# Host-side layouts for the arrays of a hybrid encoder step, and the place of the weight splits during its recurrence

## The chip, the cores and the metric

The kernel runs on one core of a Trainium2 chip, as one program and one launch. The metric is the device time of one execution in microseconds (us). The kernel before was run three times: 2982.29, 2989.22 and 2990.96 us, median 2989.22. One execution, of 2981.34 us, was recorded by the profiler, and all rows of the profile below are of that one.

## The reference

One inference step of a two-layer encoder, over a prompt of 512 tokens and a sample of 32 tokens with 1024 channels, in fp32. Each layer is: half a SwiGLU, a mixer, cross-attention to a memory of 256 tokens, half a SwiGLU; each of these ends with a LayerNorm over the scaled residual.

```python
def post_norm(x, sub, g, b):
    return layer_norm(ALPHA * x + sub, g, b)
def swiglu(x, w_up, w_down):
    gate, up = jnp.split(x @ w_up, 2, axis=-1)
    return (jax.nn.silu(gate) * up) @ w_down
```

The mixer of layer 0 is a gated linear recurrence beside chunkwise retention; that of layer 1 is RWKV-7 time mixing, a recurrence over a state of 64x64 per head and 16 heads. Outputs are the tokens, the memory's keys and values for both layers, and the states of all recurrences after the prompt and after the sample.

## The kernel before

**Layout.** Activations stand with channels on the 128 partitions: a tile is [128, 8, n], channel c*128+p at partition p of chunk c. The tokens are split into two halves, A (prompt 0 to 255, n = 256) and B (prompt 256 to 511 and the 32 of the sample, n = 288), with tiles XA, XHA, XLA and XB, XHB, XLB: the value, its rounded high part, and the rest. A matmul keeps fp32 accuracy by three passes: high weight times high x, low weight times high x, high weight times low x.

**Weights.** They are streamed in granules of 128 output columns: 1024x128 numbers, 512 KB. `_load` brings a granule by one DMA on SyncE's queue into one of three raw tiles `wr` (at most two ahead per stream). `_split` makes the two parts in one of five slots W: ScalarE the high part (L486), then VectorE (L408) or GpSimd (L412) the low one, raw minus high. `ett` chooses the engine by when a planner's clock has either free, with a lag of 300 in GpSimd's disfavour. `linear` then issues 24 matmuls for each granule and half, all through line L395.

**Order.** The program is recorded by coroutines, one for each half, one for the memory's keys and values (`mem_kv`), one for stored states. A planner gives each instruction a planned start, which becomes its priority in each engine's queue; a task with a lower `band` is placed ahead of all with a higher one. Each engine then works strictly in its own order. Lines below L500 are helpers: L395 matmul, L400 transpose by TensorE (an identity `identt` as an operand), L408 and L412 two-input operations of VectorE and GpSimd, L432 a three-input one, L443 copy, L451 memset, L486 ScalarE's activation, L491 every DMA.

**Stages.** Eight stages follow: ffn00, mix0, xa0, ffn10 of layer 0, then ffn01, mix1, xa1, ffn11. The rows of x arrive as [tokens, channels] and are transposed by TensorE in `load_x` (tiles HHA, HHB, HLB), y is transposed back in `store_x`; `mem_kv` transposes the memory, and its keys and values, with TensorE beside ffn00 and mix0; `attend` transposes the sample's cached keys; the RWKV state is transposed on its way in and out.

**The recurrence of mix1.** `wkv` cuts A and B into nine blocks: four of 64 tokens each, and the sample's 32. For each block `wkv_prep` builds small 64x64 matrices by matmuls (two chunks a block) and hands them through DRAM (`dn`) to GpSimd; `wkv_solve` is a triangular solve of 31 steps on GpSimd, two instructions a step, on tiles P and LC; the result goes through DRAM (`dz`) into tile W_114 (W_111 after the change), and `wkv_chain` carries the state on with matmuls (ax). GpSimd itself issues the DMAs P<-dn, dz<-LC and W<-dz. Meanwhile the other stages of the half that isn't in the recurrence run on with their own weight granules, through two slots, W_3 and W_4.

Of the kernel before, what the change touches and what calls it, by code (L numbers as in the profile page):

```python
# [14 lines left out]
ALU = mybir.AluOpType  # L15
# [358 lines left out]
class Kern(Clock):  # L374
# [186 lines left out]
    def setup_weights(self):  # L561
        self.slots = Res(self, [self.wslot(k) for k in range(NSLOT)])
        self.raws = Res(self, [self.pool.tile([128, 8, 128], F32, name="wr%d" % k) for k in range(NRAW)])
        self.streams, self.go = [], False
        self.kept = [0, 0]
# [37 lines left out]
    def _load(self, s):  # L603
# [10 lines left out]
        self.dma(r[:, :kc, :m], ap.rearrange("(c p) m -> p c m", p=128))  # L614
# [4 lines left out]
    def _split(self, s):  # L619
# [82 lines left out]
def load_params(K):  # L702
# [7 lines left out]
    groups = [[("ln_g", i["ln_g"].rearrange("l i (r p) -> (l i r) p", p=128), 64),  # L710
               ("ln_b", i["ln_b"].rearrange("l i (r p) -> (l i r) p", p=128), 64)]]
    one = [("mu", i["l1_mu"].rearrange("i (r p) -> (i r) p", p=128), 48)]
    for n in ("w0", "a0", "k_k", "k_a", "gn_g", "gn_b"):
        one.append((n, i["l1_" + n].rearrange("(r p) -> r p", p=128), 8))
    one.append(("r_k", i["l1_r_k"].rearrange("(r a) b -> r (a b)", a=2), 8))
    groups.append(one)
    two = [("conv_w", i["l0_conv_w"].rearrange("j (r p) -> (j r) p", p=128), 16)]
    for n in ("conv_b", "lru_ba", "lru_bx", "lru_lambda", "ret_gn_g", "ret_gn_b"):
        two.append((n, i["l0_" + n].rearrange("(r p) -> r p", p=128), 4))
    two.append(("lru0", i["state_lru0"].rearrange("b (r p) -> (b r) p", p=128), 4))  # L720
    two.append(("conv0", i["state_conv0"].rearrange("b j (r p) -> (b j r) p", p=128), 12))
    two.append(("shift1", i["state_shift1"].rearrange("b j (r p) -> (b j r) p", p=128), 8))
    groups.append(two)
    tot = sum(n for g in groups for _, _, n in g)
    K.pv = K.pool.tile([128, tot], F32, name="pv")
    col = 0
    for g in groups:
        blk = yield from K.ar.take((128,))
        st, = blk
        r = 0  # L730
        for n, ap, k in g:
            K.dma(st[r:r + k], ap)
            VEC[n] = col + r
            r += k
        ps = yield from K.aux.take()
        K.tr(ps[:, :r], st[:r])
        K.vcopy(K.pv[:, col:col + r], ps[:, :r])
        K.aux.give(ps)
        blk.free()
        col += r  # L740
# [22 lines left out]
def program(K):  # L763
# [6 lines left out]
    def add(ap, m0, m1, k0, k1):  # L770
        for m in range(m0, m1, 128):
            gran.append((ap[k0:k1, m:m + 128], (k1 - k0) // 128, 128))
# [89 lines left out]
def half_main(K, h):  # L862
# [20 lines left out]
    yield from store_x(K, h)  # L883
# [11 lines left out]
def load_x(K, h):  # L895

    nc, n = K.nc, h.n
    h.x = K.slot("X" + h.name, [128, 8, n])
    h.xh = K.slot("XH" + h.name, [128, 8, n], F32R)
    h.xl = K.slot("XL" + h.name, [128, 8, n], F32R)  # L900
    st = K.slot("HH" + h.name, [128, 8 * n])
    parts = [(K.i["x_prompt"][0, h.c0 + t * 128:h.c0 + t * 128 + 128], t * 128, 128, st[:, t * 1024:t * 1024 + 1024])
             for t in range(2)]
    if h is K.B:
        parts.append((K.i["x_sample"][0], 256, 32, K.slot("HLB", [128, 8 * n])[:, :1024]))
    for src, t0, m, st in parts:
        K.dma(st[:m], src)
    K.go = True
    yield
    for src, t0, m, st in parts:  # L910
        for q in range(2):
            ps = yield from K.aux.take()
            p3 = ps.rearrange("p (a b) -> p a b", a=4)
            for c in range(4):
                K.tr(p3[:, c, :m], st[:m, (q * 4 + c) * 128:(q * 4 + c) * 128 + 128])
            d = (slice(None), slice(q * 4, q * 4 + 4), slice(t0, t0 + m))
            K.act(h.xh[d], p3[:, :, :m])
            K.tt(h.xl[d], p3[:, :, :m], h.xh[d].bitcast(F32), ALU.subtract)
            K.vcopy(h.x[d], p3[:, :, :m])
            K.aux.give(ps)  # L920
            yield
    event(K, "x", h.name).fire(K)
    yield K.done()


def store_x(K, h):
    parts = [(K.o["y_prompt"][0, h.c0 + t * 128:h.c0 + t * 128 + 128], t * 128, 128) for t in range(2)]
    if h is K.B:
        parts.append((K.o["y_sample"][0], 256, 32))
    blks = []  # L930
    for dst, t0, m in parts:
        blk = yield from K.ar.take((1024,))
        blks.append(blk)
    for q in range(2):
        for (dst, t0, m), blk in zip(parts, blks):
            st = blk.aps[0][:m, q * 512:q * 512 + 512]
            ps = yield from K.aux.take()
            for c in range(4):
                K.tr(ps[:m, c * 128:c * 128 + 128], h.x[:, q * 4 + c, t0:t0 + m])
            (K.vcopy if t0 == 128 else K.act)(st, ps[:m])  # L940
            K.aux.give(ps)
            K.dma(dst[:, q * 512:q * 512 + 512], st)
    yield
    yield K.done()
    for blk in blks:
        blk.free()


def store_states(K):
# [5 lines left out]
    blk = yield from K.ar.take((128,))  # L955
    st, = blk
    ps = yield from K.aux.take()
    K.tr(ps[:48, :128], K.ov)
    K.vcopy(st[:48], ps[:48, :128])
    K.aux.give(ps)  # L960
    o = K.o
    yield K.done()
    for nm, a, r in (("p_conv", 0, 12), ("s_conv", 12, 12)):
        K.dma(o[nm].rearrange("b j (r p) -> (b j r) p", p=128), st[a:a + r])
    for nm, a, r in (("p_lru", 24, 4), ("s_lru", 28, 4)):
        K.dma(o[nm].rearrange("b (r p) -> (b r) p", p=128), st[a:a + r])
    for nm, a, r in (("p_shift", 32, 8), ("s_shift", 40, 8)):
        K.dma(o[nm].rearrange("b j (r p) -> (b j r) p", p=128), st[a:a + r])
    yield K.done()
    blk.free()  # L970
# [97 lines left out]
def post_ln(K, h, l, e, whole=False, final=False):  # L1068
# [53 lines left out]
def mem_kv(K):  # L1122
# [10 lines left out]
    for l in range(2):  # L1133
        for ap in (i["xa_k"][l], i["xa_v"][l]):
            for j in range(8):
                gran.append(ap[:, j * 128:j * 128 + 128])
# [7 lines left out]
    for t in range(2):  # L1144
        K.dma(st, i["mem_prompt"][0, t * 128:t * 128 + 128])
        p3 = ps.rearrange("p (a b) -> p a b", a=4)
        for q in range(2):
            for c in range(4):
                K.tr(p3[:, c], st[:, (q * 4 + c) * 128:(q * 4 + c) * 128 + 128])
            hi, lo = mh[:, q * 4:q * 4 + 4, t * 128:t * 128 + 128], ml[:, q * 4:q * 4 + 4, t * 128:t * 128 + 128]  # L1150
            K.act(hi, p3)
            K.tt(lo, p3, hi.bitcast(F32), ALU.subtract)
# [4 lines left out]
    for g, ap in enumerate(gran):  # L1157
# [3 lines left out]
        dst = K.o["mem_v" if kind else "mem_k"][l, 0].rearrange("(t p) h d -> p t (h d)", p=128)  # L1161
# [920 lines left out]
```

## Time and profile before

| | |
|---|---|
| runs | 2982.29, 2989.22, 2990.96 us |
| profiled execution | 2981.34 us, of which the span of the trace is 2979.5 us |
| mean granted TensorE clock | 0.952 |
| TensorE busy in 1000 to 1300 us | 300.00 of 300 us |
| TensorE busy in 1300 to 1500 us | 192.04 of 200 us |
| TensorE busy in 1500 to 1850 us | 338.79 of 350 us |
| GpSimd busy, all | 909.1 us, 424.20 of them between 1850 and 2450 us |
| HBM traffic, mean | 110 GB/s |

Engines are PE (TensorE's matmuls), PEld (its weight loads), DVE (VectorE), ACT (ScalarE), POOL (GpSimd) and SP (SyncE). A row of a view by groups names the line, engine, operation, what is written <- what is read, the shape and the count, then busy us and the mean ns of one, then the idle time of that engine just before these instructions and what ended it. Neighbouring matmuls overlap, so a group's busy time is less than count times mean. A row of the timeline gives start and length in us, and in brackets the idle time ahead of it with its releaser. A row of the chain of waits gives a start, a length and what that piece of the end's path was spent on. The recurrence lies between about 1880 and 2440 us.

### The profile page before, as it was taken

The page shows a single profiled execution, that of the slowest core. Times are in us where ns is not written, and L with a number is a line of the kernel's source. Part 1 is how long each engine was busy: PE and PEld are TensorE (multiplying, and loading weights), DVE is VectorE, ACT ScalarE, POOL GpSimd, SP SyncE. Part 2 cuts the span into 40 slices and gives each one's busy share as a digit, 9 for nine tenths or more (in the row PEclk, how much of TensorE's full clock was granted, in tenths as well). Part 3 has the DMA queues.
Part 4 walks back from the last instruction along what each step waited for, and adds up shares of the span by engine and source line. Part 5 has one row for each costly group of instructions (what it writes and reads, how often), then busy time and mean ns, then how long its engine had stood idle before and what let it go on. Part 6 is the DMA issues. An engine that isn't in the chain of part 4 may idle for free.

```text
span 2979.5 us, 54689 instructions
## 1 busy us (share of the span) xinstructions
PE 2809.6 (94%) x22456; PEld 2701.7 (91%) x22456; DVE 1765.9 (59%) x3094; ACT 1276.8 (43%) x2182; POOL 909.1 (31%) x1201
## 2 busy tenths in 40 slices
PE   8999998999998999998999899799779989999998
PEld 8999998898898999998999899578678878999997
DVE  5333436677767333356345655877588657765665
ACT  4323233665555222234234443444345454654444
POOL 2000104433314000023001212588577764241311
PEclk9999999999999999999999999799678889999999
DMA  6443443223232332322346554133122245546563
GB/s 184 124 120 116 134 117 107 77 75 90 89 98 71 100 89 82 93 79 85 86 138 184 143 145 128 38 90 98 42 70 80 75 115 167 149 144 181 167 174 94
DMA packets 611035, 330.56 MB, mean 111 GB/s; under 512 B 29032, under 2 KB 603840, under 8 KB 610784
## 3 DMA queue, kind: packets, MB, share of 16 engines
q1 hardware_dynamic: 603328, 310.93, 36.3%
q0 software_dynamic: 7456, 16.13, 2.0%
q8 instruction: 176, 2.88, 0.4%
q14 instruction: 75, 0.61, 0.1%
HBM read 313.09 MB, written 13.92 MB: 110 GB/s over the span
## 4 chain that ended last, share of the span: by engine, by line
PE 71%; DVE 11%; POOL 7%; ACT 5%; issue 3%; DMA 3%; SPq 0%; DVEq 0%; ACTq 0%; POOLq 0%
PE mm L395 65%; PE ax L395 5%; POOL LC L412 2%; POOL P L412 2%; DVE W L408 2%; ACT arena L486 2%; DVE arena L408 1%; DVE arena L432 1%; ACT W L486 1%; PE ax L400 1%; DVE XA L408 1%; DMA wr<-in_ffn_up 1%; POOL arena L412 1%; ACT L2043 1%; DVE XB L408 1%
## 5 line engine op out<-in xcount | busy, mean ns | idle before, releaser
L486 ACT ACTIVATE W<-wr 128x1024 fp32r<-128x1024 f32 (+1 forms) x558 | 577.7, 1038 | 725.8 <-PE mm L395 587.1
L408 DVE TENSOR_TENSOR W<-wr,W 128x1024 fp32r<-128x1024 f32 (+1 forms) x453 | 562.4, 1244 | 541.2 <-ACT W L486 536.8
L395 PE MATMUL mm<-XHB,W 128*128 128x288 f32 x3840 | 581.0, 300 | 15.4 <-ACT XHB L486 4.8
L395 PEld LDWEIGHTS mm<-XHB,W 128*128 128x128 f32 x3840 | 528.3, 190 | 24.1 <-ACT XHB L486 5.8
L395 PE MATMUL mm<-XHA,W 128*128 128x256 f32 x3840 | 530.8, 288 | 16.4 <-ACT XHA L486 6.6
L395 PEld LDWEIGHTS mm<-XHA,W 128*128 128x128 f32 x3840 | 494.8, 193 | 25.9 <-ACT XHA L486 10.8
L412 POOL TENSOR_TENSOR W<-wr,W 128x1024 fp32r<-128x1024 f32 (+1 forms) x105 | 253.9, 2419 | 659.7 <-ACT W L486 652.7
L395 PE MATMUL mm<-XLB,W 128*128 128x288 f32 x1984 | 313.6, 298 | 1.4 <-DVE XLB L408 1.4
L395 PE MATMUL mm<-HHB,W 128*128 128x288 f32 x1920 | 291.6, 302 | 9.7 <-ACT W L486 3.5
L395 PE MATMUL mm<-XLA,W 128*128 128x256 f32 x1984 | 290.5, 285 | 2.3 <-POOL XLA L412 2.3
L395 PE MATMUL mm<-HHA,W 128*128 128x256 f32 x1920 | 271.7, 290 | 14.5 <-DVE XA L408 5.0
L395 PEld LDWEIGHTS mm<-XLB,W 128*128 128x128 f32 x1984 | 281.2, 190 | 3.4 <-DVE XLB L408 1.9
L395 PEld LDWEIGHTS mm<-HHB,W 128*128 128x128 f32 x1920 | 268.7, 192 | 12.8 <-ACT W L486 4.5
L395 PEld LDWEIGHTS mm<-HHA,W 128*128 128x128 f32 x1920 | 250.7, 194 | 20.5 <-ACT W L486 5.3
L395 PEld LDWEIGHTS mm<-XLA,W 128*128 128x128 f32 x1984 | 261.6, 191 | 4.5 <-POOL XLA L412 2.5
L486 ACT ACTIVATE arena<-mm 128x256 f32<-128x256 f32 (+4 forms) x292 | 112.6, 388 | 308.2 <-PE mm L395 289.9
L432 DVE SCALAR_TENSOR_TENSOR arena<-mm,arena 128x288 f32<-128x288 f32 (+1 forms) x176 | 77.3, 439 | 161.7 <-PE mm L395 143.7
L395 PE MATMUL mm<-HLB,W 128*128 128x288 f32 x896 | 142.7, 299 | 0.0
L395 PE MATMUL mm<-HLA,W 128*128 128x256 f32 x896 | 129.9, 284 | 0.0
L412 POOL TENSOR_TENSOR SUMA<-XA 128x256 f32<-128x256 f32 x16 | 14.4, 901 | 377.3 <-DVE XA L408 360.7
L395 PEld LDWEIGHTS mm<-HLB,W 128*128 128x128 f32 x896 | 129.3, 192 | 0.1
L412 POOL TENSOR_TENSOR LC<-LC,P 128x66 f32<-128x66 f32 (+24 forms) x279 | 122.7, 440 | 20.6
(430 smaller groups left out, 3769.6 us busy)
## 6 DMA issues: line engine op xcount, KB each, us to landing
wr<-in_ffn_up SPq DMA_DIRECT2D x246, 512.0 KB
wr<-in_ffn_down SPq DMA_DIRECT2D x96, 448.0 KB
wr<-in_l_w_rkv SPq DMA_DIRECT2D x48, 512.0 KB
wr<-in_ffn_down SPq DMA_DIRECT2D x40, 512.0 KB
wr<-in_l_w_in SPq DMA_DIRECT2D x24, 512.0 KB
wr<-in_l_w_out SPq DMA_DIRECT2D x24, 512.0 KB
wr<-in_xa_q SPq DMA_DIRECT2D x24, 512.0 KB
wr<-in_xa_o SPq DMA_DIRECT2D x24, 512.0 KB
```

The source lines that it names most:

```text
L395: self.nc.tensor.matmul(out, lhsT, rhs, start=start, stop=stop)
L400: self.nc.tensor.transpose(out, in_, self.ident[k0:k0 + k, k0:k0 + k])
L408: self.nc.vector.tensor_tensor(out, a, b, op=op)
L412: self.nc.gpsimd.tensor_tensor(out, a, b, op=op)
L432: self.nc.vector.scalar_tensor_tensor(out, a, s, b, op0=op0, op1=op1)
L486: return self.nc.scalar.activation(out, a, f, bias=bias, scale=scale, **kw)
L2043: nc.scalar.preload_act_table_set(name)
```

## The change

Two parts. First, arrays are laid out on the host as the DMAs want them, before the launch and after it: a weight granule is contiguous, with 4 KB for each partition instead of eight pieces of 512 bytes; x, the memory, the vectors, the cached keys, the small RWKV weights and the RWKV state come as they stand in SBUF; y, the memory's keys and values, the small states and the RWKV state are stored as they stand there. The transposes of these by TensorE, and the copies behind them, are left out; those of the memory's values stay, since attention needs values in both layouts. Second, between the start and the end of `wkv`'s tasks (`K.busy`) a split is recorded with band -1, and its low part is always VectorE's.

```diff
         ap, kc, m = g[k][:3]
         self.end = self.now
-        self.dma(r[:, :kc, :m], ap.rearrange("(c p) m -> p c m", p=128))
+        self.dma(r[:, :kc, :m], ap)
...
+        band = self.band
+        if self.busy:
+            self.band = -1
         self.act(wh[:, :kc, :m], r[:, :kc, :m])
-        self.ett(wl[:, :kc, :m], r[:, :kc, :m], wh[:, :kc, :m].bitcast(F32), ALU.subtract, GSP)
+        if self.busy:
+            self.tt(wl[:, :kc, :m], r[:, :kc, :m], wh[:, :kc, :m].bitcast(F32), ALU.subtract)
+        else:
+            self.ett(wl[:, :kc, :m], r[:, :kc, :m], wh[:, :kc, :m].bitcast(F32), ALU.subtract, GSP)
+        self.band = band
...
-    yield from store_x(K, h)
...
-            for c in range(4):
-                K.tr(p3[:, c, :m], st[:m, (q * 4 + c) * 128:(q * 4 + c) * 128 + 128])
...
+    for c in range(0, 8, 2):
+        (K.dma, K.adma)[c // 2 % 2 if h is K.A else 0](h.x[:, c:c + 2], K.i["x"][:, c:c + 2, h.c0:h.c0 + n])
     K.go = True
     yield
...
+    for c in range(0, 8, 2):
+        u = slice(c, c + 2)
+        K.act(h.xh[:, u], h.x[:, u])
+        K.tt(h.xl[:, u], h.x[:, u], h.xh[:, u].bitcast(F32), ALU.subtract)
+        yield
...
             first(c)
             second(c)
+            if final:
+                K.dma(K.o["y"][:, c, h.c0:h.c0 + n], x[:, c])
...
         K.act(a, ps[:, :256])
+        K.gdma(K.o["mem_v" if kind else "mem_k"][l, j * 128:j * 128 + 128], a)
         if kind == 0:
             K.gdma(K.kt[l][j * 128:j * 128 + 128], a)
+            yield K.done()
+            continue
...
-        K.dma(r3[:, 0], K.i["cache_mem_k"][l, 0, :, hd].rearrange("(c p) d -> p c d", p=128))
+        K.dma(r3[:, 0], K.i["cache_k"][l, hd])
...
+    K.busy = True
     evs = [K.spawn(f(K, w), 0, p)
            for f, p in ((wkv_prep, -1), (wkv_solve, -2), (wkv_load, -3), (wkv_chain, -4), (wkv_norm, -1))]
     for e in evs:
         yield e
+    K.busy = False
...
-                yield from state_out(K, w, Yn, K.o["p_wkv"][0])
+                K.gdma(K.o["p_wkv"], Yn[0:64])
```

What this moves is seen in the order of the instructions. On TensorE at the program's start, before:

```order
L400 MATMUL ax_67<-identt,HHA_93 128x128 x4
L400 MATMUL ax_69<-identt,HHA_93 128x128 x4
L400 MATMUL ax_70<-identt,HHA_93 128x128 x4
L400 MATMUL ax_67<-identt,HHA_93 128x128 x4
L395 MATMUL mm_63<-XHA_91,W_1_71 128x256
L400 MATMUL ax_68<-identt,HHB_101 128x128 x4
L400 MATMUL ax_69<-identt,HHB_101 128x128 x4
L395 MATMUL mm_64<-XHA_91,W_2_72 128x256
L395 MATMUL mm_63<-XHA_91,W_1_71 128x256 x15
```

and of the change, at the same place:

```order
L395 MATMUL mm_63<-XHA_91,W_1_71 128x256 x16
L395 MATMUL mm_63<-XLA_92,W_1_71 128x256 x8
L395 MATMUL mm_64<-XHA_91,W_2_72 128x256 x16
L395 MATMUL mm_64<-XLA_92,W_2_72 128x256 x8
L395 MATMUL mm_65<-XHB_100,W_1_71 128x288 x16
```

The transposes of x ahead of and between the first linears are gone; the first granules are used whole, one after the other.

On GpSimd behind the solve of the recurrence's first block, where its result is handed on (dz, then W_114) and the next block's matrices are fetched (P<-dn), before:

```order
L412 TENSOR_TENSOR LC_7380<-LC_7380,P_115_17677 128x8
L491 DMA dz_17682<-LC_7380 256x1x32 x4
L412 TENSOR_TENSOR W_3_73<-wr_76,W_3_73 128x1024
L412 TENSOR_TENSOR W_4_74<-wr_77,W_4_74 128x1024
L491 DMA W_114_17676<-dz_17682 32x8x32 x4
L451 MEMSET LC_7380 128x256
L491 DMA P_115_17677<-dn_17681 32x1024 x4
L451 MEMSET LC_7380 32x8 x4
L412 TENSOR_TENSOR W_4_74<-wr_77,W_4_74 128x1024
L412 TENSOR_TENSOR P_115_17677<-LC_7380,P_115_17677 128x31
```

and of the change:

```order
L412 TENSOR_TENSOR LC_7233<-LC_7233,P_112_17512 128x8
L491 DMA dz_17517<-LC_7233 256x1x32 x4
L491 DMA W_111_17511<-dz_17517 32x8x32 x4
L451 MEMSET LC_7233 128x256
L491 DMA P_112_17512<-dn_17516 32x1024 x4
L451 MEMSET LC_7233 32x8 x4
L412 TENSOR_TENSOR P_112_17512<-LC_7233,P_112_17512 128x31
```

The three splits of weights have left GpSimd's queue. Behind the second and the third solve something else is moved as well: P<-dn stood ahead of dz<-LC there and now stands behind W<-dz.

On TensorE where the recurrence passes from half A to half B: the matmuls on W_111, W_110 (64x64) are the preparation of B's first block, one tile for each of its two chunks, and `ax<-arena,W_114` is the use of the last solve of A. Before:

```order
L395 MATMUL mm_64<-W_111_17673 64x64 x4
L395 MATMUL mm_66<-W_111_17673 64x64 x7
L395 MATMUL ax_68<-wr_78,W_110_17672 32x64 x16
L395 MATMUL ax_68<-arena_79,W_114_17676 128x64 x4
L395 MATMUL ax_69<-wr_78,W_110_17672 64x64 x16
L395 MATMUL ax_68<-W_110_17672,wr_78 64x32 x16
L395 MATMUL mm_64<-W_110_17672 64x64
L395 MATMUL mm_66<-W_110_17672 64x64
L395 MATMUL ax_67<-HLA_16848,centt 128x512
L395 MATMUL mm_64<-W_110_17672 64x64 x7
```

and of the change, where the two chunks stand in W_108 and XHB, and W_111 is the solve's result:

```order
L395 MATMUL mm_63<-W_108_17508 64x64 x7
L395 MATMUL mm_66<-W_108_17508 64x64 x7
L395 MATMUL mm_63<-XHB_19937 64x64 x8
L395 MATMUL mm_66<-XHB_19937 64x64 x8
L395 MATMUL ax_69<-wr_76,W_107_17507 32x64 x16
L395 MATMUL mm_63<-arena_79,bonest 128x512
L395 MATMUL mm_66<-arena_79,bonest 128x512
L395 MATMUL ax_69<-arena_79,W_111_17511 128x64 x4
```

The second chunk's preparation stood behind the second use of the solve's result and now stands ahead of it.

More of the change, by code (lines that the diff above doesn't have):

```diff
@@ L563, in setup_weights @@
         self.raws = Res(self, [self.pool.tile([128, 8, 128], F32, name="wr%d" % k) for k in range(NRAW)])
-        self.streams, self.go = [], False
+        self.streams, self.go, self.busy = [], False, False
         self.kept = [0, 0]
@@ L709, in load_params @@
     K.dma(K.cent, K.c["cent"])
[L710 to L740, printed above, removed]
+    K.pv = K.pool.tile([128, i["pv"].shape[1]], F32, name="pv")
+    K.dma(K.pv, i["pv"])
     K.lng2 = K.pool.tile([128, 64], F32, name="lng2")
@@ L954, in store_states @@
     yield event(K, "shift", "B")
[L955 to L970, printed above, removed]
+    K.dma(K.o["ov"], K.ov)
 def ffn(K, h, l, e):
@@ L1143, in mem_kv @@
     st, = blk
[L1144 to L1152, printed above, removed]
+    for q in range(2):
+        u = slice(4 * q, 4 * q + 4)
+        s4 = st.rearrange("p (c t) -> p c t", c=4)
+        K.dma(s4, i["mem"][:, u])
+        K.act(mh[:, u], s4)
+        K.tt(ml[:, u], s4, mh[:, u].bitcast(F32), ALU.subtract)
         yield K.done()
@@ L1253, in attend @@
     ks = yield from K.keys.take()
-    if c0 == 0:
-        K.act(ks[:, 0], raw[:, 0])
-        K.tt(ks[:, 1], raw[:, 0], ks[:, 0].bitcast(F32), ALU.subtract)
-    else:
-        ps = yield from K.aux.take()
-        p3 = ps.rearrange("p (c n) -> p c n", c=2)
-        for a in range(2):
-            for b in range(2):
-                K.tr(p3[:, b, a * 128:a * 128 + 128], r3[:, 0, a, b * 128:b * 128 + 128])
-        K.act(ks[:, 0], ps)
-        K.tt(ks[:, 1], ps, ks[:, 0].bitcast(F32), ALU.subtract)
-        K.aux.give(ps)
+    K.act(ks[:, 0], raw[:, 0])
+    K.tt(ks[:, 1], raw[:, 0], ks[:, 0].bitcast(F32), ALU.subtract)
     t = K.done()
@@ L1933, in wkv_load @@
         event(K, "load", ci).fire(K)
-def state_out(K, w, Y, dst):
-    blk = yield from K.ar.take((16, 64))
-    st, = blk
-    for q in range(2):
-        ps = yield from w.pl.take()
-        for g in range(8):
-            K.tr(ps[0:64, g * 64:g * 64 + 64], Y[0:64, 8 * q + g])
-        K.act(st[0:64, 8 * q:8 * q + 8], ps[0:64].rearrange("p (g k) -> p g k", g=8))
-        w.pl.give(ps)
-    K.gdma(dst.rearrange("h v k -> v h k"), st[0:64])
-    yield K.done()
-    blk.free()
 def wkv_chain(K, w):
@@ L1959, in wkv_chain @@
         if L == 32:
-            blk = yield from K.ar.take((16, 64))
-            st, = blk
-            yield K.ready([st])
-            K.dma(st[0:64], K.i["state_wkv1"][0].rearrange("h v k -> v h k"))
-            yield K.done()
-            for q in range(2):
-                for g in range(8):
-                    K.tr(b1[0:64, g * 64:g * 64 + 64], st[0:64, 8 * q + g])
-                K.act(Y[0:64, 8 * q:8 * q + 8], b1[0:64].rearrange("p (g k) -> p g k", g=8))
-            blk.free()
+            yield K.ready([Y[0:64]])
+            K.dma(Y[0:64], K.i["wkv0"])
         yield event(K, "load", ci)
@@ L2067 @@
     arrays, ins, outs, consts = {}, {}, {}, {}
-    for name in INS:
-        a = np.ascontiguousarray(inputs[name])
+    for name, a in lay(inputs).items():
+        a = np.ascontiguousarray(a)
         arrays["in_" + name] = a
@@ L2080 @@
     r = run(nc, [arrays], core_ids=[0])
-    return tuple(r.results[0]["out_" + name] for name, _ in OUTS)
+    return tuple(np.ascontiguousarray(a) for a in unlay({name: np.asarray(r.results[0]["out_" + name]) for name, _ in OUTS}))
```

114 lines of the change are left out of this document (57 added, 57 removed), and 3 rows, old and new, of the table INS.

## The prediction

> **What bounds the kernel now.** I read the page's busy shares and chain of waits first, then a table by stages, because a share of the span says little where the limits change from stage to stage.
>
> ```profile
> PE 2809.6 (94%) x22456; PEld 2701.7 (91%) x22456; DVE 1765.9 (59%) x3094; ACT 1276.8 (43%) x2182; POOL 909.1 (31%) x1201
> ...
> q1 hardware_dynamic: 603328, 310.93, 36.3%
> ...
> PE 71%; DVE 11%; POOL 7%; ACT 5%; issue 3%; DMA 3%; SPq 0%; DVEq 0%; ACTq 0%; POOLq 0%
> ```
>
> TensorE is busy 94% and holds 71% of the chain. So what leaves TensorE counts, but only where TensorE is what everything else waits for. The table by stages (stretch, its length, then busy us and instructions of PE, PEld, DVE, ACT, POOL, then clock, DMA share and GB/s) says where:
>
> ```profile
> 0.00:50.00 50.00, 42.31 (x311) 41.02 (x311) 25.44 (x50) 22.39 (x33) 11.18 (x9) 0.97 0.78 226
> 50.00:500.00 450.00, 450.00 (x3607) 449.84 (x3606) 186.71 (x276) 138.50 (x217) 64.45 (x80) 1.00 0.41 119
> 500.00:1000.00 500.00, 464.91 (x3507) 449.63 (x3507) 354.55 (x907) 270.60 (x543) 162.01 (x159) 0.96 0.30 86
> ...
> 1850.00:2450.00 600.00, 521.57 (x4736) 447.74 (x4736) 446.53 (x789) 284.79 (x521) 424.20 (x796) 0.83 0.27 74
> 2450.00:2950.00 500.00, 482.95 (x3733) 477.04 (x3733) 325.53 (x458) 252.70 (x384) 129.73 (x76) 0.99 0.56 160
> ```
>
> From 50 to 500 us TensorE has no gap: work taken from it there is time won, one for one. From 1850 to 2450 us, the recurrence, it is idle for 78.4 us and the clock is down to 0.83; GpSimd and VectorE are at 424 and 447 of 600, so several engines take turns. All idle time of TensorE comes to 2979.5 - 2809.6 = 170 us, the most that waits can give back.
>
> **The change, transposes first.** The groups of L400 by shape (busy us, mean ns | idle before):
>
> ```profile
> L400 PE MATMUL ax<-identt,arena 128*128 128x128 f32 x129 | 22.1, 280 | 1.7 <-DMA arena<-in_cache_mem_k 1.7
> L400 PE MATMUL mm<-identt,arena 128*128 128x128 f32 x80 | 14.7, 273 | 0.0
> L400 PE MATMUL ax<-identt,XA 128*128 128x128 f32 x16 | 2.6, 283 | 0.8 <-ACT XA L486 0.7
> L400 PE MATMUL ax<-identt,Q 64*64 64x64 f32 x16 | 2.1, 311 | 4.4 <-DVE Q L408 3.7 <-ACT arena L486 0.7
> L400 PE MATMUL ax<-identt,arena 64*64 64x64 f32 x16 | 1.7, 247 | 0.0
> ```
>
> - Of the 80 that write mm, the memory's 16 and the keys' 32 go, the values' 32 stay: 48 x 14.7/80 = 8.8 us, nearly all in the full stretch before 500 us. I take **-8.8**.
> - Cached keys: 32 of the 129 at 22.1/129 = 0.171 us are 5.5 us, in stretches that are 93 and 97% full (464.91 and 482.95 of 500); with the 1.7 us wait the bounds are 0 and -7.2. I take **-3.5**.
> - RWKV state: 16 and 16 of the last two rows, 3.8 us with 4.4 us of waits, and 16 more of the second output, which fall in a wait for weights. Bounds 0 and -8.2; **-3**.
> - Vectors and small states: three transposes at about 0.27, **-0.5**.
> - Half A's y: 16 transposes, 2.6 us, just ahead of a full stretch: **-2.6**, bounds 0 and -3.4.
>
> The copies that go with them ran on VectorE and ScalarE, which have room in these stages, and I cost them at nothing.
>
> **Start and end.** TensorE's timeline at the start, then rows of the end (start, length, what, and the idle time ahead):
>
> ```profile
> 5.21 2.79 PE L400 MATMUL ax<-identt,HHA 128*128 128x128 f32 x12 [5.21 <-DMA HHA<-in_x_prompt]
> ...
> 12.17 1.03 PE L395 MATMUL mm<-XHA,W 128*128 128x256 f32 x4
> ...
> 2969.18 4.64 ACT L486 ACTIVATE XB<-XB,pv,lng 128x288 f32<-128x288 f32 x8 [2.00 <-DVE XB L408]
> 2975.56 0.59 ACT L486 ACTIVATE arena<-ax 32x512 f32<-32x512 f32 x1 [0.24 <-PE ax L400]
> 2976.28 0.41 SPq L491 DMA_DIRECT2D out_y_sample<-arena  x1
> ```
>
> x has landed at 5.21, while linears run in a row only from 12.17. Without the transposes x needs a split on ScalarE and VectorE, some 2 us, so the linears start near 7: **-5**, bounds -7 (at landing) and 0 (the first weights, which share the queue with x, come no sooner). At the end the last XB is written at 2969.18 + 4.64 = 2973.82, and the last store is issued at 2976.28. With y stored from XB that issue moves to about 2973.9: **-2.4**, bounds 0 and -3.
>
> **Weight transfers.** In the chain of waits 13 pieces are a weight granule under way, 59.0 us together; the first, the longest and the last (start, length):
>
> ```profile
> 600.15 5.17 DMA wr<-in_l_w_in
> ...
> 1744.83 5.48 DMA wr<-in_ffn_up
> ...
> 2665.94 4.73 DMA wr<-in_ffn_up
> ```
>
> The queue's row gives 310.93 MB in 603328 packets, 515 bytes each, and 0.363 x 16 x 2979.5 us / 603328 = 28.7 ns of an engine for each. A granule is 1024 such packets, 64 for each of 16 engines: 1.84 us of a piece of 4.5 us. That is what larger packets can shorten; the rest is latency and other loads. Bounds: 0, and 13 x 1.84 = -24 if packets cost nothing. I take a quarter, **-6**.
>
> The Trainium skill, "DMA: Bandwidth & Descriptors", section "Specifications", puts the smallest transfer at line rate at 512 bytes, with about 27 GiB/s for each engine; by that this term would be 0 and the forecast 6 us longer. The trace speaks against it: 515 bytes in 28.7 ns are 18 GB/s.
>
> **The recurrence.** Groups of the window from 1880 to 2440 us, and the shares of the chain there:
>
> ```profile
> L412 POOL TENSOR_TENSOR LC<-LC,P 128x66 f32<-128x66 f32 (+24 forms) x279 | 122.7, 440 | 20.6
> L412 POOL TENSOR_TENSOR P<-LC,P 128x66 f32<-128x66 f32 (+24 forms) x279 | 115.2, 413 | 23.3 <-DMA P<-dn 3.4
> ...
> L408 DVE TENSOR_TENSOR W<-wr,W 128x1024 fp32r<-128x1024 f32 x40 | 53.5, 1341 | 28.0 <-ACT W L486 27.9
> ...
> L412 POOL TENSOR_TENSOR W<-wr,W 128x1024 fp32r<-128x1024 f32 x14 | 33.8, 2413 | 13.2 <-ACT W L486 13.2
> ```
>
> ```profile
> by line: PE mm L395 20.9%; PE ax L395 11.1%; POOL LC L412 10.0%; POOL P L412 10.0%; issue 9.1%; DVE W L408 2.8%; DVE arena L432 2.6%; DVE arena L408 2.4%; ACT arena L486 2.3%; PE ax L400 2.2%; DVE arena L455 1.8%; POOL arena L412 1.5%; ACT
> ```
>
> The solver's two groups are 237.9 us long and 20% of 560 us = 112 us of the chain, so a us of the solver is worth 112/237.9 = 0.47 us of the end. GpSimd's timeline shows what the splits do to it:
>
> ```profile
> 1936.63 2.33 POOL L491 DMA_DIRECT2D dz<-LC  x4 [0.29 <-POOL LC L412]
> 1938.88 2.47 POOL L412 TENSOR_TENSOR W<-wr,W 128x1024 fp32r<-128x1024 f32 x1
> ...
> 1958.34 2.54 POOL L412 TENSOR_TENSOR W<-wr,W 128x1024 fp32r<-128x1024 f32 x1 [9.20 <-ACT W L486]
> ...
> 2109.37 2.33 POOL L491 DMA_DIRECT2D W<-dz  x4
> ...
> 2145.47 2.01 POOL L491 DMA_DIRECT2D P<-dn  x4 [15.41 <-DMA dn<-W]
> ```
>
> - **Splits leave GpSimd.** The 14 splits and their waits are 33.8 + 13.2 = 47.0 us; in one case the solver stood still for 9.20 us behind a split whose high part wasn't there. Some five stand between dz<-LC and W<-dz, where GpSimd would wait for a DMA anyway (as at 1938.88), 12.4 us, so 34.6 us come off the solver. Against it, 14 more splits on VectorE at 1.341 us, 18.8 us, whose effect on the solver is in the next rows. Net (-34.6 + 18.8) x 0.47 = **-7.4**; bounds +9 and -34.6.
>
> ```profile
> 1995.83 0.93 POOL L412 TENSOR_TENSOR LC<-LC,P 128x24 f32<-128x24 f32 x1
> ...
> 1995.59 0.71 DVE L408 TENSOR_TENSOR Q<-Q,pc 64x512 f32<-64x512 f32 x1
> ...
> 2102.58 0.23 POOL L412 TENSOR_TENSOR LC<-LC,P 128x24 f32<-128x24 f32 x1
> ```
>
> The same step of the solve takes 0.23 us with VectorE idle and 0.93 beside a two-input VectorE operation of 0.71: the solver waits for about one such operation whole. So a split moved to VectorE is not gone for GpSimd, and I charged all 1.341 us of each.
>
> The Trainium skill, "SBUF — State Buffer", section "SBUF: two separate sides", says why: the pair of ports is an exclusive lock, and a VectorE operation with two SBUF inputs and a GpSimd operation that reads SBUF shut each other out for a whole instruction. The rows agree (0.93 - 0.23 = 0.70 beside 0.71). By that rule alone, with none of the saved waits on the path, the edit would cost 9 us.
>
> - **P<-dn behind W<-dz.** After two solves the next block's fetch is issued behind dz<-LC and W<-dz, 2.33 us each: 2 x 4.66 x 0.47 = **+4**, bounds 0 and +9.
> - **Weights sooner.** A low part takes 1.341 us in place of 2.413 and is urgent; TensorE's waits for GpSimd's W are 2.5 us: **-2.5**, bounds 0 and -15 (the groups of linears wait 5.2 and 9.8 us in all). What the urgent splits push back on VectorE is the last rival.
> - **From A to B.** Between 2104 and 2148 us the solver has nothing to do: the 15.41 us in the last row of the timeline are a wait for the second chunk's dn, whose matmuls stand behind a use of the solve just ended. In the changed order they stand ahead of it. I take the wait whole, **-15**; bounds 0 (some other input of B's first block is late next) and -39 (the whole gap but the DMAs).
>
> The recurrence together: -7.4 + 4 - 2.5 - 15 = -21.
>
> **Sum.** -8.8 - 3.5 - 3 - 0.5 - 2.6 - 5 - 2.4 - 6 - 21 = -52.8. Against the profiled execution that is 2981.3 - 52.8 = 2928.5; this lies 7.9 below the median of the runs shown, 2989.2, and against the median it is 2936.
>
> **Rivals.**
> - *The waits go further.* The gap from A to B closes whole (24 us more), weight transfers lose 12 us more and VectorE's split costs the solver nothing (9 us more): 2936 - 45 = 2891. For it: 59 us of weight waits, the 9.20 us stop. Against it: half of a solver's us was not on the chain.
> - *The recurrence gains nothing*, because VectorE's splits hold the solver up as at 1995.83 for what they save, and the gap from A to B has another cause: 21 us less won, and the weight term 0: 2936 + 27 = 2963. The more of the solver runs beside a VectorE as full as at 1995, the likelier this is.
> - *The saved time of TensorE is given back*: what the transposes free is lost again in waits for the next granule, as no engine supplies weights faster. Only start and end remain, 5 + 2.4: 2989.2 - 7.4, about 2982. Against it: TensorE runs 450.00 of 450 us beside the same supply, so the supply has room there.
> - *Slower.* The 54 splits (40 + 14) now go ahead of what `wkv_prep` and the state's chain have on VectorE, which is 447 of 600 us full. Each that delays the chain by all of its 1.341 us adds that; all of them 72 us. With no other gain in the recurrence it decides once the 32 us won outside are eaten, at 24 splits of 54 (47 us, 35 splits, if the turn's 15 us are won). With three in four of the 54 landing, 54 us: 2936 + 21 + 54 = 3011. Against it: VectorE's W has 2.8% of the chain now, 16 us.
>
> **How the numbers follow.** Chances: forecast 0.50 (its own range 2912 to 2957), waits go further 0.17, recurrence gains nothing 0.19, given back 0.08, slower 0.06. A measurement of this kernel can tell about 0.3% from no change, 9 us: faster is below 2980. Faster 0.50 + 0.17 + 0.19 = 0.86; within 0.3% 0.08; slower 0.06. The range from 2888 to 2981 leaves out the slower case, about half of the one given back, and the low half of the first rival, under 0.2.
>
> **What would show it.** In the profile after: the first stretch of linears before 8 us; 32 in place of 80 transposes into mm and a stretch to 500 us that stays full; the last store within 0.1 us of the last XB; pieces of weights in the chain well under 59.0 us; no W on POOL between 1880 and 2440 and solver steps with a mean under 440 and 413 ns (over 460 would speak for VectorE's splits holding them up); no 15 us wait for dn at the turn to B. The prediction is wrong if TensorE's idle time of 78 us in the recurrence doesn't shrink, or if TensorE waits there for VectorE's other results more than now.

## The result and the profile after

The changed kernel takes 2960.93 us (median of four runs, 2959.93 to 2962.34) beside 2988.2 us before: 27 us less, a ratio of 0.9911 with a 95% interval of 0.9895 to 0.9926. The profiled execution took 2960.97 us, its span is 2959.2. The forecast was 2936 with a range of 2888 to 2981; its direction held, its size was twice the measured one. The time is near that of the second rival, in which the recurrence gains nothing (2963).

The page after, its engines, its DMA queue and its chain:

```profile
PE 2792.9 (94%) x22244; PEld 2683.3 (91%) x22244; DVE 1764.9 (60%) x3082; ACT 1270.2 (43%) x2165; POOL 857.2 (29%) x1175
...
q1 hardware_dynamic: 109776, 310.41, 34.5%
...
PE 73%; DVE 9%; POOL 8%; ACT 4%; issue 3%; DMA 2%; SPq 0%; DVEq 0%; ACTq 0%; POOLq 0%
```

The table by stages after, with the columns of the one shown before:

```profile
0.00:50.00 50.00, 40.04 (x300) 39.75 (x301) 28.34 (x66) 27.21 (x37) 5.97 (x7) 1.00 0.69 229
50.00:500.00 450.00, 449.60 (x3601) 448.67 (x3599) 189.40 (x240) 138.92 (x216) 82.14 (x90) 1.00 0.39 121
...
1850.00:2450.00 600.00, 520.76 (x4670) 443.12 (x4670) 447.14 (x801) 279.26 (x510) 387.40 (x772) 0.82 0.26 74
```

GpSimd is busy 37 us less in the recurrence, and yet TensorE is idle there as long as before: 79.2 us against 78.4. Where the 27 us come from shows in two landmarks of the chain of waits that both programs have, a run of 60 matmuls near the start of mix1 and a long one of linears behind the recurrence (start, length), before and after:

```profile
1708.00 12.95 PE ax L395 x60
...
2611.18 47.60 PE mm L395 x375
```

```profile
1690.85 12.95 PE ax L395 x60
...
2596.43 47.61 PE mm L395 x374
```

17.2 us are won by the first, from start-up, the transposes of layer 0 and weight transfers, and 14.8 us by the second. So between the two the change loses 2.4 us, where it was to win 21 in the recurrence alone.

For the comparison of many kernels I use a **stage time**: of the 558 high parts of splits on ScalarE, the time from the start of the 313th to that of the 457th (1731.6 and 2630.5 us before). It holds the recurrence and what stands around it, and the same work in every kernel; it is read from each kernel's one profiled execution. Before it is 898.9 us, after 897.0: its ends lie elsewhere than the two landmarks, but by it, too, next to nothing is won. One execution is not the median. With the late rule, below, it is the lowest of four (2938.65 us beside a median of 2943.13), with urgent splits on any engine the highest (2965.70 beside 2962.31); so a few us of a stage time mean little.

The gaps between solves show where the forecast's terms of the recurrence went. GpSimd's timeline after, around the end of the third solve:

```profile
2013.72 0.65 POOL L412 TENSOR_TENSOR LC<-LC,P 128x8 f32<-128x8 f32 x1
2014.67 2.37 POOL L491 DMA_DIRECT2D dz<-LC  x4 [0.30 <-POOL LC L412]
2019.11 2.31 POOL L491 DMA_DIRECT2D W<-dz  x4 [2.06 <-PE mm L395]
2021.41 0.92 POOL L451 MEMSET LC<- 128x256 f32 x5
2045.10 2.00 POOL L491 DMA_DIRECT2D P<-dn  x4 [22.76 <-DMA dn<-W]
...
2050.79 0.69 POOL L412 TENSOR_TENSOR P<-LC,P 128x31 f32<-128x31 f32 x1
```

The solver ends at 2014.37 and starts again at 2050.79. In between GpSimd stands still for 22.76 us until the fourth block's matrices (dn) are there. This gap of 36.4 us was 15.7 us before (2054.1 to 2069.8). The gap from A to B, on which the forecast counted, did shrink, from 45.8 to 35.3 us.

### The profile page after: what moved, and what is told of

It is laid out like the page before. It is cut to its first block, busy times and chain, and to the rows that moved or that the text cites. A ratio compares the mean times of both kernels' runs of the same rounds, so it can differ in the third digit from the quotient of the medians.

```text
span 2959.2 us, 54175 instructions
## 1 busy us (share of the span) xinstructions
PE 2792.9 (94%) x22244; PEld 2683.3 (91%) x22244; DVE 1764.9 (60%) x3082; ACT 1270.2 (43%) x2165; POOL 857.2 (29%) x1175
## 3 DMA queue, kind: packets, MB, share of 16 engines
q1 hardware_dynamic: 109776, 310.41, 34.5%
## 4 chain that ended last, share of the span: by engine, by line
PE 73%; DVE 9%; POOL 8%; ACT 4%; issue 3%; DMA 2%; SPq 0%; DVEq 0%; ACTq 0%; POOLq 0%
PE mm L395 68%; PE ax L395 5%; POOL LC L412 3%; POOL P L412 3%; DVE W L408 2%; DVE arena L408 1%; ACT arena L486 1%; ACT W L486 1%; DVE arena L432 1%; DVE XB L408 1%; PE ax L400 1%; DVE XA L408 1%; DMA wr<-in_ffn_up 1%; ACT L1938 1%; ACT XHA L486 1%
## 5 line engine op out<-in xcount | busy, mean ns | idle before, releaser
L408 DVE TENSOR_TENSOR W<-wr,W 128x1024 fp32r<-128x1024 f32 (+1 forms) x473 | 584.7, 1238 | 540.6 <-ACT W L486 539.7
L412 POOL TENSOR_TENSOR W<-wr,W 128x1024 fp32r<-128x1024 f32 (+1 forms) x85 | 207.0, 2437 | 655.3 <-ACT W L486 613.8
L486 ACT ACTIVATE arena<-mm 128x256 f32<-128x256 f32 (+3 forms) x292 | 112.8, 388 | 296.2 <-PE mm L395 277.6
L412 POOL TENSOR_TENSOR P<-LC,P 128x66 f32<-128x66 f32 (+24 forms) x279 | 121.8, 437 | 33.6 <-DMA P<-dn 13.8
```

The lines of the kernel that those rows point to most:

```text
L408: self.nc.vector.tensor_tensor(out, a, b, op=op)
L412: self.nc.gpsimd.tensor_tensor(out, a, b, op=op)
L486: return self.nc.scalar.activation(out, a, f, bias=bias, scale=scale, **kw)
```

## The experiments

**First four: which part does what.** The layouts alone (the split rule left out):

```diff
-        band = self.band
-        if self.busy:
-            self.band = -1
         self.act(wh[:, :kc, :m], r[:, :kc, :m])
-        if self.busy:
-            self.tt(wl[:, :kc, :m], r[:, :kc, :m], wh[:, :kc, :m].bitcast(F32), ALU.subtract)
-        else:
-            self.ett(wl[:, :kc, :m], r[:, :kc, :m], wh[:, :kc, :m].bitcast(F32), ALU.subtract, GSP)
-        self.band = band
+        self.ett(wl[:, :kc, :m], r[:, :kc, :m], wh[:, :kc, :m].bitcast(F32), ALU.subtract, GSP)
```

> The layouts alone; splits during the recurrence are chosen by the planner as before. Theory (the layouts give all of the 27 us, the split rule gives nothing): 2955 to 2966 us, with the solver's sequence from its first step to its last at 510 +- 8 us. Rival (the split rule gives some 10 us or more, the layouts the rest): 2970 to 2980 us. Second rival (the split rule costs, by VectorE holding up the solver): 2940 to 2953 us.

Measured: 2948.49 us, 0.9871 of before (0.9849 to 0.9894). By its time it is the second rival: the layouts give 38 us, and the rule takes some 12 back. The rival's reason, VectorE holding up the solver, doesn't follow from the time. The solver's sequence from its first step to its last takes 496.8 us, not the 510 of the theory; it took 510.2 before and 513.1 in the change.

The kernel before with the rule alone (the same lines, put into it):

> The kernel before with the split rule alone. Theory (the rule gives nothing): within 7 us of before. Rival (it gives 10 or more): 2970 to 2980 us. Second rival (it costs): 2995 us or more. If layouts and rule add up, this and e1 together explain the 27 us.

Measured: 2995.42, ratio 1.0027 (1.0014 to 1.004): 9 us slower, or 16.8 by the stage time (915.7 against 898.9). That is just inside the second rival; this order, too, is slower with the rule. But the solver's sequence is not longer here, 508.6 us against 510.2, though its third gap is 37.5 us. What is lost stands behind the last solve: from there to the end of the stage it takes 238.4 us, 217.5 before.

The rule was then taken apart. VectorE alone but not urgent:

```diff
-        if self.busy:
-            self.band = -1
```

> Layouts, and VectorE alone for the low parts during the recurrence, but not urgent. If urgency is what pushes the preparation back (waits for dn of 49 us in the changed kernel), those waits fall under 35 us and the time is 2945 to 2956 us. If the preparation is late for another reason, the time is within 5 us of the changed kernel's 2961.

Measured: 2954.76, ratio 0.9895 (0.9874 to 0.9917), within the first theory's time. But its condition failed: the waits for dn did not fall under 35 us (P<-dn had 54.9 us of idle time ahead of it). So the time doesn't show that urgency pushes the preparation back. The third gap fell to 11.7 us, and the gap from A to B grew to 52.1.

Urgent, but with the engine left to the planner:

```diff
-        if self.busy:
-            self.tt(wl[:, :kc, :m], r[:, :kc, :m], wh[:, :kc, :m].bitcast(F32), ALU.subtract)
-        else:
-            self.ett(wl[:, :kc, :m], r[:, :kc, :m], wh[:, :kc, :m].bitcast(F32), ALU.subtract, GSP)
+        self.ett(wl[:, :kc, :m], r[:, :kc, :m], wh[:, :kc, :m].bitcast(F32), ALU.subtract, GSP)
```

> Layouts, splits urgent during the recurrence, but the planner may give low parts to GpSimd. If GpSimd's splits in the solver's way are what cost (34.6 us of its time, 0.47 of it on the chain), this is 8 to 16 us slower than the changed kernel. If VectorE's splits hold the solver up by as much, it is within 5 us of it.

Measured: 2962.31, ratio 0.9916 (0.989 to 0.9941): within 2 us of the change. Nine splits are GpSimd's again, and that makes no difference to the time. Of the rule's two halves the urgency looks like the costly one: 2962.31 us with it alone, 2954.76 with VectorE alone, 2948.49 with neither. These steps of 6 to 14 us have to be weighed against what another order alone does, further below.

**Where the urgency costs.** The rule from the end of A's last block on, and up to it:

```diff
-    K.busy = True
     evs = [K.spawn(f(K, w), 0, p)
...
             if b == 3:
                 K.qt.give("Q1", "P0")
+                K.busy = True
```

> Layouts, and the split rule only from the end of half A's last block on (blocks 5 to 9). Theory (the rule costs where it fills the gap between the third and the fourth solve with linears, 36 us against 9 with the layouts alone): that gap goes back under 20 us and the time is 2944 to 2953, near the layouts alone. Rival (the cost of the rule is spread over all blocks): 2953 to 2959.

> Layouts, and the split rule only up to the end of half A's last block. Theory: the gap between the third and fourth solve stays over 30 us and the time is 2956 to 2965, like the whole change. Rival (spread over all blocks): 2951 to 2957.

(In the second, `K.busy = True` stays where it was, and the line added is `K.busy = False`.) Measured: late 2943.13, ratio 0.9856 (0.984 to 0.9872), third gap 9.7 us; early 2972.15, ratio 0.9948 (0.9931 to 0.9965), third gap 38.7. The place is as the theory had it, half A; late is 1 us under the range it gave, and the price of early is above it, 11 us more than that of the whole rule. The solver around the third gap with the late rule:

```profile
2031.11 0.21 POOL L412 TENSOR_TENSOR LC<-LC,P 128x8 f32<-128x8 f32 x1
...
2034.00 2.02 POOL L491 DMA_DIRECT2D P<-dn  x4
...
2041.03 0.45 POOL L412 TENSOR_TENSOR P<-LC,P 128x31 f32<-128x31 f32 x1
```

This is worth reading beside the rows after. With the rule on A the third solve ends 17 us **earlier** (2014.4 against 2031.3); with the late rule four splits of 2.36 to 2.47 us stand on GpSimd by then, and here none; the first three solves take 101.5 us, with the late rule 119.2 and before the change 112.2. That is what the forecast expected. But the next solve starts 10 us **later** (2050.8 against 2041.0), because its dn is late. The preparation on TensorE has become the wait. TensorE itself was not waiting there. Windows of the change, then of the late rule:

```profile
1985.00:1990.00 5.00, 5.00 (x23) 3.08 (x24) 0.92 (x2) 0.00 (x0) 3.98 (x14) 0.82 0.07 30
1990.00:2020.00 30.00, 30.00 (x161) 21.57 (x162) 18.53 (x34) 9.96 (x17) 24.96 (x48) 0.50 0.09 23
```

```profile
1980.00:1990.00 10.00, 10.00 (x33) 7.25 (x34) 5.38 (x13) 2.50 (x7) 5.25 (x18) 0.52 0.08 16
1990.00:2015.00 25.00, 23.82 (x220) 21.28 (x220) 21.59 (x33) 15.13 (x26) 15.65 (x24) 0.97 0.28 85
```

After the change TensorE is busy for 30.00 of 30 us, at a granted clock of 0.50, and gets through 161 matmuls. With the late rule it has a stretch at half clock as well, but of 10 us, and then 220 matmuls in 25 us, at 0.97. In the 35 us of each pair of windows it is 184 against 253. What it does there, in its timeline after:

```profile
1984.60 0.32 PE L395 MATMUL ax<-Q,W 64*64 64x64 f32 x2
1984.85 0.40 PE L395 MATMUL mm<-XHB,W 128*128 128x288 f32 x1
1985.18 0.33 PE L395 MATMUL ax<-Q,W 64*64 64x64 f32 x2
...
1993.86 1.92 PE L395 MATMUL ax<-W,Q 128*64 128x32 f32 x32
1995.71 2.40 PE L395 MATMUL mm<-SUMA,LC 64*128 64x64 f32 x20
1998.04 1.33 PE L395 MATMUL mm<-XHB,W 128*128 128x288 f32 x4
1999.17 3.51 PE L395 MATMUL ax<-TGA,LC 128*128 128x64 f32 x16
...
2003.31 0.61 PE L395 MATMUL mm<-XHB,W 128*128 128x288 f32 x1
2003.85 0.42 PE L395 MATMUL ax<-wr,W 96*32 96x64 f32 x2
2004.19 0.61 PE L395 MATMUL mm<-XHB,W 128*128 128x288 f32 x1
...
2019.65 1.06 PE L400 MATMUL ax<-identt,VA 128*32 128x128 f32 x4
2020.36 2.03 PE L395 MATMUL mm<-XHB,W 128*128 128x288 f32 x7
```

The urgent splits have linears ready while the planner is laying out the preparation, and it deals them out one by one between its small matmuls: to 1992 us, and again from 2002 to 2017. (A pair in the trace, as x2 here, is one matmul of the program: the trace shows these small fp32 ones as two records each.) One pair and one linear take 0.58 us (1984.60 to 1985.18) at full clock and 0.88 us (2003.31 to 2004.19) at half. The same things in a row are cheap; the late rule's timeline has both:

```profile
1994.52 2.28 PE L395 MATMUL mm<-XHB,W 128*128 128x288 f32 x16
...
2006.68 1.15 PE L395 MATMUL ax<-Q,W 64*64 64x64 f32 x32
```

That is 2.28/16 = 0.14 us for a linear's matmul and 2 x 1.15/32 = 0.07 for a pair, 0.21 together: an alternation wastes some 0.37 us at full clock. From 1984.85 us on 25 linears stand alone like this; at 0.37 each they delay TensorE by some 9 us, an estimate, where the gap grew by 20.7. The half clock, which lengthens all else in the stretch, is the other delay that the rows show.

**How far is it luck of an order?** The layouts alone with the planner's lag for GpSimd at 330 instead of 300 (`GSP = 330.0`), which means nothing to the chip:

> The layouts alone with the planner's lag against GpSimd at 330 instead of 300: another order for a constant that means nothing to the chip. It measures how far a time moves with the order alone. If the cost of the split rule (12 us) is more than luck of an order, this is within 5 us of the layouts alone (2943 to 2954); if it is 2955 or more, one order differs from another by as much as the rule.

Measured: 2939.73, ratio 0.9842 (0.9826 to 0.9858): the lowest median of all, 3 us below what was expected, and 9 below the layouts alone by another order (the intervals of the two overlap a little). The rule's cost of 12 us is hardly more than that. The same lag with the late rule:

> Layouts, the split rule from the end of half A's last block on, and the lag of 330. If the two gains over the layouts alone (5 us from the late rule, 9 from the lag) add up: 2932 to 2937. If both are luck of an order: 2938 to 2950.

Measured: 2944.87, ratio 0.9855 (0.9833 to 0.9876). The gains don't add up; by the expectation both are luck of an order.

**The planner's clock.** The theory says that the planner deals linears too early because it takes TensorE for faster than it is. The rule kept, matmuls costed longer:

```diff
             cost = 4 * (max(n, 62) / 2.4) + 2
+        if self.busy:
+            cost *= 1.2
         self.plan("pe", cost, [out], [lhsT, rhs])
```

> The whole change, with matmuls costed 1.2 times as long in the planner's clock during the recurrence, about what the granted clock of 0.82 makes of them; nothing else. Theory (linears stand ahead of the preparation in the third gap because splits come early and the planner takes TensorE for faster than it is): that gap of 36 us falls under 25 and the time is 2940 to 2955. Rival (the rule's cost has nothing to do with where the linears stand): 2957 to 2967 with the gap over 30 us.

> Layouts alone with the lag of 330 and matmuls costed 1.2 times as long in the planner's clock during the whole of K.busy (the flag stands, the split rule is not there). If the planner's clock of TensorE is what costs in the recurrence: 2925 to 2936. If it is only another order: 2937 to 2950.

Measured: with the rule 2953.75, ratio 0.9888 (0.9873 to 0.9904), third gap 14.7 us, but 89.4 us from A to B. With the layouts alone 2977.54, ratio 0.9971 (0.996 to 0.9982), where the gap from A to B is 104.5 us. So with the rule the third gap closes and the time is in the range of the theory, and another gap opens: in it TensorE runs 128 matmuls of B's linears and 192 of A's (25 and none in the change). That gap is not time lost as a whole, since TensorE is busy for 77 of its 89 us. The kernel without the rule missed both of its ranges, by 27 us and more. The cure is not one.

**Two terms by themselves.** The weight granules back in pieces of 512 bytes; every engine's order is that of the change:

```diff
-            gran.append((ap[m // 128, :, k0 // 128:k1 // 128], (k1 - k0) // 128, 128))
+            gran.append((ap[k0:k1, m:m + 128].rearrange("(c p) m -> p c m", p=128), (k1 - k0) // 128, 128))
...
-                gran.append(ap[j])
+                gran.append(ap[:, j * 128:j * 128 + 128].rearrange("(c p) m -> p c m", p=128))
```

> The whole change, with the weight granules alone in their old layout in DRAM (pieces of 512 bytes); the order of all instructions is that of the change. Forecast's term: 6 us slower than the change (2964 to 2970). Rival (pieces of 512 bytes cost nothing that anything waits for): within 3 us of the change's 2961. Second rival (larger pieces are what the layouts gain): 2975 or more.

Measured: 2968.83, ratio 0.9945 (0.9929 to 0.9961): 7.9 us slower than the change. The view of tile `wr` on SyncE, for pieces of 512 bytes and then for the change, gives who waited for a granule in all, and the times from issue to landing:

```profile
ACT W L486: 118.0, 61
...
DMA to landing us min/median/max: 3.4/3.9/7.4
```

```profile
ACT W L486: 84.9, 54
...
DMA to landing us min/median/max: 3.1/3.6/8.7
```

With large pieces a granule lands 0.3 us sooner at the median, ScalarE waits 33 us less, and the end comes 7.9 us sooner. How the one becomes the other is not shown. Of the 7.5 us between the two profiled executions 1.3 are there by the start of the stage (1713.4 against 1714.7 us), and 5.7 arise in it (897.0 against 902.7). There TensorE isn't idle for longer with the small pieces (85.6 us against 88.1), but busy for longer with the same matmuls in the same order (817.0 against 808.9).

The transposes of the memory's keys put back, with the copies behind them:

```diff
         if kind == 0:
             K.gdma(K.kt[l][j * 128:j * 128 + 128], a)
-            yield K.done()
-            continue
...
         K.vcopy(b, p3)
+        if kind == 0:
+            yield K.done()
+            continue
```

> The whole change with the 32 transposes of the memory's keys and the 16 copies behind them put back (their result isn't stored). Forecast's term: 32 x 14.7/80 = 5.9 us of the -8.8, so that the layer-1 stages start 5 to 7 us later than in the change. Rival (TensorE's transposes there fall beside waits): they start within 2 us of it. The total is not read for this, since the order in the recurrence is another one.

Measured: the landmark of 60 matmuls starts at 1696.27 us instead of 1690.85, 5.4 us later, as the term had it. Its total, 2958.17 (ratio 0.9899, 0.9879 to 0.9919), is **not** later, and that became the most useful result: it has the whole split rule, but in another order, in which the third gap is 13.8 us. Its stage time is 886.6 us, as with the layouts alone.

**All of them together.** Alternations are counted in TensorE's records over the whole trace: a linear, and then one to six records of 64 columns or fewer (three fp32 matmuls) before something else. Gaps are from the end of one solve to the start of the next.

| kernel | split rule | stage time | alternations | third gap | gap A to B |
|---|---|---|---|---|---|
| before | no | 898.9 | 41 | 15.7 | 45.8 |
| before with the rule | all | 915.7 | 69 | 37.5 | 41.8 |
| layouts alone | no | 886.5 | 39 | 9.3 | 43.4 |
| the same, lag 330 | no | 878.9 | 42 | 9.3 | 43.2 |
| late rule | on B | 875.0 | 46 | 9.7 | 42.4 |
| late rule, lag 330 | on B | 881.2 | 46 | 9.9 | 45.6 |
| VectorE alone | not urgent | 891.1 | 71 | 11.7 | 52.1 |
| the change | all | 897.0 | 61 | 36.4 | 35.3 |
| urgent, any engine | urgent | 902.2 | 76 | 37.8 | 31.3 |
| early rule | on A | 909.9 | 74 | 38.7 | 35.4 |
| rule, keys put back | all | 886.6 | 35 | 13.8 | 37.6 |
| rule, cost 1.2 | all | 888.8 | 23 | 14.7 | 89.4 |
| layouts, cost 1.2 | no | 916.7 | 39 | 10.5 | 104.5 |

Of the kernels with the layouts and without a gap of 80 us or more, those with 35 to 46 alternations take 875 to 887 us, those with 61 to 76 take 891 to 910. The windows of the stage show where the difference lies, for the layouts alone, the change, the early rule and the rule with the keys put back (busy us of TensorE first, then the other engines, clock last but two):

```profile
1713.47:2599.97 886.50, 800.97 (x6912) 724.99 (x6911) 648.88 (x1077) 437.34 (x772) 471.81 (x829) 0.88 0.34 103
1713.35:2610.31 896.96, 808.90 (x6912) 725.40 (x6911) 645.20 (x1092) 436.20 (x771) 459.87 (x814) 0.88 0.34 102
1713.04:2622.99 909.95, 825.93 (x6912) 734.84 (x6911) 643.65 (x1077) 434.00 (x768) 490.14 (x832) 0.87 0.33 101
1720.25:2606.88 886.63, 787.93 (x6912) 712.38 (x6911) 640.11 (x1092) 436.54 (x772) 457.60 (x814) 0.90 0.35 103
```

TensorE takes 788 to 826 us for the same 6912 matmuls, while its idle time is 85.5, 88.1, 84.0 and 98.7 us. So the slower of them are slower mostly because the same work keeps TensorE busy for longer, and not because it waits for longer. Some of that needs no other order: with pieces of 512 bytes the change's order took 817.0.

The rule as such is on both sides: 61 alternations and 897.0 in the change, 35 and 886.6 in the kernel with the keys' transposes. That speaks for a cost that comes with the order that the rule brings about, and against a cost of VectorE's time or of the rule by itself. It is argued, not shown: one kernel stands on the good side, the groups are 4 us apart in single executions, and no run changes the alternations alone. Nor is urgency needed for them: VectorE alone, not urgent, has 71.

## Why the prediction was right, and where not

- **Start-up, -5**: right in size. By the 13th granule's split the change is 5.2 us ahead (61.3 against 66.5 us). The route was another: linears run in a row from 10.54 us, not near 7, because the first weights, whose transfer takes 5.96 us from 2.18, hold them up and not x. What is won is that nothing interrupts them then: of 311 matmuls in the first 50 us 51 were transposes, of the 300 now none. So the size was met by another route than the one it was worked out by, which is luck.
- **Memory's transposes, -8.8**: right; for the keys alone 5.4 us measured beside 5.9.
- **Cached keys and vectors, -4**: not measured alone. Layer 0 as a whole (to the 169th split) is 16.6 us shorter; start, memory, vectors and half of the cached keys make 16.
- **Weight transfers, -6**: 7.9 us measured. Its working was worse than its size: of the large packets I expected a higher rate. The queue's row after gives 2828 bytes a packet and 0.345 x 16 x 2959.2 / 109776 = 149 ns, 19 GB/s for an engine, beside 18 before. So the Trainium skill's rule ("DMA: Bandwidth & Descriptors", section "Specifications") that 512 bytes are enough for line rate agrees with these packets in that larger ones hardly move faster; the 0 that was worked out from it doesn't hold, as a granule still lands 0.3 us sooner. What makes that, no run here shows. The chain, from which the term came, has 8 pieces of weights under way now, 35.4 us in place of 59.0; with pieces of 512 bytes in the same order it has 11 and 57.7, and with the layouts alone 4 and 17.8, so the order moves them as well.
- **RWKV state, -3**: not measured alone, and as far as the chain shows given back. The transposes went, but the state's load now stands on the path: matmuls of the last block wait 7.3 us for it, and the chain has this piece:

```profile
2400.21 3.59 DMA Q<-in_wkv
```

- **A's y, -2.6**: nothing. The tail from the 457th split to the last is 316.2 us, 315.0 before. The step that failed is "just ahead of a full stretch". Before, the transposes filled a wait of TensorE for ScalarE; after, the same wait is bare. TensorE's first linear behind it, before and after:

```profile
2857.08 2.38 PE L395 MATMUL mm<-XHB,W 128*128 128x288 f32 x16 [1.28 <-ACT arena L486]
```

```profile
2829.97 3.12 PE L395 MATMUL mm<-XHB,W 128*128 128x288 f32 x16 [3.61 <-ACT arena L486]
```

- **End, -2.4**: right. From the last XB to the span's end it was 2979.5 - 2973.8 = 5.7 us, and is now 2959.2 - 2956.2 = 3.0. The last rows of ScalarE and SyncE after:

```profile
2951.55 4.63 ACT L486 ACTIVATE XB<-XB,pv,lng 128x288 f32<-128x288 f32 x8 [2.00 <-DVE XB L408]
2952.20 4.34 SPq L491 DMA_DIRECT2D out_y<-XB  x8
```

- **The recurrence, -21: this is the step that failed.** The sum took a shorter solver (-7.4), the turn from A to B (-15) and sooner weights (-2.5) and let nothing else become late. The first three solves are shorter by 10.7 us, the turn by 10.5, but the third gap grew by 20.7. At the turn the second chunk's preparation does stand ahead now, and still a wait for dn is left, of 12.15 us where it was 15.41:

```profile
2125.20 2.02 POOL L491 DMA_DIRECT2D P<-dn  x4 [12.15 <-DMA dn<-XHB]
```

The solver's groups as a whole are longer:

```profile
L412 POOL TENSOR_TENSOR LC<-LC,P 128x66 f32<-128x66 f32 (+24 forms) x279 | 124.8, 447 | 20.6
L412 POOL TENSOR_TENSOR P<-LC,P 128x66 f32<-128x66 f32 (+24 forms) x279 | 121.8, 437 | 33.6 <-DMA P<-dn 13.8
```

The means of 440 and 413 ns before have become 447 and 437, under the 460 named for the rival in which VectorE's splits hold the solver up. With all low parts on VectorE but none urgent they are 424 and 399, below those of before, so the 18.8 us charged for this are not to be seen there; that no solver step is held up by a split is not shown either. The rows behind the charge were read too simply: the VectorE operation at 1995.59 ends at 1996.30, 0.47 us after the solver's step at 1995.83 began, so it can't account for all of the 0.70 us. The term that was missing is TensorE in that gap, which was put at nothing without a reason: at "Splits leave GpSimd" I asked what a us of the solver is worth, and not what the preparation then lacks. In its place the runs showed GpSimd waiting 22.76 us for the fourth block's matrices, whose preparation stood among linears on a TensorE that was busy all the time. The forecast named a wait for VectorE's results as the thing that might grow; it was the preparation's own matmuls.
- **The signs.** The forecast named TensorE's idle time in the recurrence, 78 us, as what would show it wrong if it didn't shrink. It didn't: 79.2. Of the others, the linears do not run before 8 us, and the solver's steps did not become shorter; 32 transposes into mm are left, the stretch to 500 us stays full (449.60 of 450), and no W stands on GpSimd in the recurrence. So most of the layouts' terms came true, and that of the recurrence did not.
- **The rivals.** "The recurrence gains nothing" came true in its number, not in its reason. It took the weight term as 0, and that is 7.9; the layouts gave 12.4 us in the stage (898.9 to 886.5), and the rule took 10.5 back. "Slower" did not come true. Its thought that urgent splits push something back fits the third gap, but what waits there is TensorE's work, not VectorE's.

## What to carry to other kernels

Making a helper's work urgent can also bring forward everything that waits for it: here the linears, which were then dealt between the small matmuls of the very chain that the urgency was to serve. Ahead of a change of priorities, look at the instruction order of the engine that consumes the result, count where long and short matmuls alternate one by one, and price an alternation from a row that has it. And before a difference of 10 us is put down to a rule in a planned kernel, run one other order of the same kernel: here two constants of the planner, without meaning to the chip, moved the layouts alone by 9 us down and from there by 38 up.

## What the runs showed of the hardware

TensorE can show no idle time and still have a granted clock of 0.50: for 30 us in the windows above (busy 30.00 of 30 us, as the records have it). The Trainium skill, "TensorE: Matmul & The Clock Gate", section "Part 1: The HAM clock gate (the "warmup" mystery)", says that some 3.4 us of sustained activity release the clock; the 30.00 of 30 us at 0.50 differ from that, and the measurement decides. What the gate counts as activity, no run here shows.

The alternation can't be the whole reason. It begins at 1984.60 us, at a clock of 1.00; the clock falls between 1988 and 1989. It stays at 0.50 from 1993.86 to 2002.44 us as well, where nothing alternates one by one: small matmuls stand there in rows of 16 to 32 records, with four linears between them. It rises between 2022 and 2023 us, behind rows of five, five and seven linears from 2017.08 on; with the late rule between 1989 and 1990, where eight linears stand in a row from 1987.84. That small matmuls, alone or in turn with linears, keep the clock down is argued from these places, and no run here shows it by itself.

Matmuls of two shapes in turn cost more than the same ones in rows: 0.58 us for a linear and a pair at full clock, where rows of their own make 0.21.
